# Seven-product values in an encoder layer: the first product's bank copies and the first keys' copies change places

## The chip, the cores and the metric

The kernel runs on 1 core of one Trainium2 chip. The metric is device time in microseconds (us) of one execution. In the text PE is TensorE (matmuls), ACT is ScalarE, DVE is VectorE, POOL is GpSimd, SP is the engine that issues most transfers. A bank is one PSUM tile of 128 partitions by 512 float32.

## The reference, cut to what matters

The program is a two-layer encoder over 512 tokens of width 1024. The change lies in layer 0, in the input projection of the neighbourhood attention, which makes queries, keys, values and a gate from the normed tokens `xn`:

```python
def mixer_na(xn, w_in, rpb, w_out):
    B, S, _ = xn.shape
    hd = NA_HEADS * NA_HEAD_DIM
    q, k, v, z = jnp.split(xn @ w_in, 4, axis=-1)
    shp = (B, S, NA_HEADS, NA_HEAD_DIM)
    o = neighbourhood_attention(q.reshape(shp), k.reshape(shp), v.reshape(shp), rpb)
    return (o.reshape(B, S, hd) * jax.nn.silu(z)) @ w_out
```

After it come the gated per-layer embedding, a second layer with latent attention, and a last norm. All of that is the same in both kernels.

## The kernel before, in words

Every float32 operand of a matmul is split in two parts, `hi` (a rounded copy, cast by ACT) and `lo` (what is left, subtracted by DVE or POOL), and a product is three kinds of matmul: hi by hi, lo by hi, hi by lo. So a weight tile costs a load (SP), a cast (ACT) and a subtraction (DVE in `piece`, line 240, POOL in `load_w`, line 89). Both write through three buffers each of `wraw`, `whi` and `wlo`.

`values_seven` makes the values with seven block products instead of eight. Products 1, 2 and 4 take quarters of the transposed tokens as they stand; products 7, 5, 6 and 3 take mixes of quarters. A mix (`mix`, line 255) is a DVE sum in place on the tokens (`xT<-xT`, 128x1024), an ACT cast (`V<-xT`) and a DVE subtraction (`V<-xT,V`). The mixes 6 and 3 hang together: the sum of 3 reads what the sum of 6 wrote. The weights of products 7, 6 and 4 are made in one tile `W7` by adding further pieces to it one after the other (`sums`, seen as `W<-W,wraw`).

A product is 24 matmuls on two banks, in four blocks of six: first chunk on bank 0, first chunk on bank 1, second chunk on bank 0, second chunk on bank 1. Products 1, 7 and 6 open two banks each (kinds `S`, `T` and `mm`); 2 goes on in the banks of 1, 4 in those of 7, 5 and 3 in those of 6. So before product 2 writes, the result of product 1 must be copied out: `after1(0)` and `after1(1)`, two ACT copies `s<-ps_S`. In the same way `after6` copies out of the banks of 6 (`s<-ps_mm`) before product 5 writes them, and `after7` adds to those of 7 and copies them.

Between the products stand the queries and keys of the first two head pairs, 0 and 1: `pair.load(j)` brings two weight tiles with `load_w`, `pair.products(j)` is 48 matmuls (24 for queries, 24 for keys) on the two `mm` banks, `pair.queries(j)` and `pair.keys(j)` are the copies out of these banks: for keys four ACT copies (`da` twice, `db` twice) and two DVE subtractions (`la`, `lb`). There are only two `mm` banks: the keys of pair 1 take the bank of the keys of pair 0, product 6 takes those of pair 1.

The order on ACT and DVE of all calls through `self.act` and `self.dve` is the order in which `values_seven` writes them (class `InOrder`, whose line 51 therefore stands beside all of them in the profile). The casts of `load_w` (line 100) go past this class, and a scheduler places them. The matmuls of the products stand in written order too (line 302 in the profile for the seven products, line 407 for queries and keys).

Of the kernel before, what the change touches and what calls it, by code (L numbers as in the profile page):

```python
# [56 lines left out]
class Trunk:  # L57
# [209 lines left out]
    def values_seven(self, pool, xT, xk, Q, pair, more):  # L267
# [14 lines left out]
        def left(p, s, k, i):  # L282
            if p in X:
                return X[p][:, 2 * s + k // 2, k % 2 * 256 + i * P:k % 2 * 256 + (i + 1) * P]
            half, t = {1: (0, i), 2: (1, i), 4: (1, 2 + i)}[p]
            return xT[s][half][:, k, t * P:(t + 1) * P]
# [4 lines left out]
        def product(p):  # L291
            for i in range(2):
                if p in banks:
                    C[p, i] = self.psum(banks[p])
            for c in range(2):
                for i in range(2):
                    ps = C[base.get(p, p), i]
                    m = [(left(p, s, k, i), W[p][c][r][:, k % 2 * S:(k % 2 + 1) * S])
                         for s, r in ((0, 0), (1, 0), (0, 1)) for k in (2 * c, 2 * c + 1)]
                    for j, (l, r) in enumerate(m):  # L300
                        with self.tc.issue_after(self.last_mm.ins):
                            self.last_mm = nc.tensor.matmul(ps, l, r, start=c == 0 and j == 0 and p in banks,  # L302
                                                            stop=c == 1 and j == 5 and p in (2, 3, 4),
                                                            skip_group_check=True)
# [4 lines left out]
        def copy(name, i, ps):  # L309
            t = kept(name, i)  # L310
            self.act.activation(t, ps, AF.Copy)
            return t
# [4 lines left out]
        def after1(i):  # L317
            s1[i] = copy("s1", i, C[1, i])
# [18 lines left out]
        def mixed(p):  # L337
            X[p], rest = self.mix(xk, p)
            return rest
# [8 lines left out]
        pair.queries(0)  # L348
        rest5 = mixed(5)
        product(1)  # L350
        p21 = self.piece(None, self.raw_piece(0, 3))
        rest5()
        W[2].append(p21())
        rest6 = mixed(6)
        pair.keys(0)
        pair.load(1)
        rest6()
        mixed(3)()
        more()
        after1(0)  # L360
        after1(1)
        made(7, 0, T[7][:, 0, :], True)
        product(2)
        out(0, 0, 0, C[1, 0])
# [1086 lines left out]
```

## Time and profile before

| | |
|---|---|
| median of 3 runs | 673.18 us (672.94 to 673.78) |
| the profiled execution, own time | 673.3 us |
| its span, first to last instruction | 671.5 us |
| outside the span | 1.8 us |
| PE busy in the span | 644.4 us (96%) |
| ACT, DVE, POOL busy | 451.5, 441.1, 413.3 us |
| mean granted PE clock | 0.982 |

In rows of the timeline the first number is the start in us from the span's start, the second the duration in us, then engine, line, operation, output<-inputs, and xN for N instructions merged in one row. In square brackets is the time for which the engine sat idle before the row, and what released it. A row of the windows view gives start:end, length, then for each engine its busy time and, in brackets, how many instructions ran; at the end stand the granted PE clock, the busy share of the transfer engines and GB/s.

### The profile page before, as it was taken

What the parts mean: (1) busy time and instruction counts of PE and PEld (TensorE: products, weight loads), DVE (VectorE), ACT (ScalarE), POOL (GpSimd) and SP (SyncE); (2) the same over time, 40 slices, a digit from 0 to 9 for tenths busy, and PEclk for the clock granted to TensorE, in tenths of its full rate; (3) what the DMA queues carried; (4) which work ended last, traced back from release to release, by engine and by line L of the source; (5) the groups of instructions that cost most, each with busy time, mean ns of one, the idle gap of its engine ahead of it and who ended that gap; (6) DMA issues with size and microseconds to landing.
All of it is one profiled execution on the core that took longest, in us unless ns stands there. A gap on an engine that the chain in (4) does not pass through costs nothing.

```text
span 671.5 us, 9963 instructions
## 1 busy us (share of the span) xinstructions
PE 644.4 (96%) x3299; PEld 544.2 (81%) x3299; DVE 441.1 (66%) x898; ACT 451.5 (67%) x887; POOL 413.3 (62%) x373
## 2 busy tenths in 40 slices
PE   9996599998999999999999999999999999999994
PEld 6884488787888888888899888888888888888884
DVE  6197587467787652667861723688888886474675
ACT  7574455686877774378754544887989898536855
POOL 0463101775887874389844744685978978436974
PEclk9998699998999999999999999999999999999997
DMA  9849344655995897745644425320121213583524
GB/s 331 330 160 287 104 138 129 221 131 163 231 244 166 217 246 201 280 158 188 192 149 130 138 71 148 96 68 9 56 64 63 64 48 125 191 327 126 173 78 157
DMA packets 46131, 107.41 MB, mean 160 GB/s; under 512 B 4736, under 2 KB 17792, under 8 KB 46080
## 3 DMA queue, kind: packets, MB, share of 16 engines
q1 hardware_dynamic: 34608, 87.12, 38.7%
q0 software_dynamic: 11040, 18.88, 13.2%
q10 hardware_dynamic: 432, 0.79, 0.3%
q8 instruction: 26, 0.43, 0.3%
q14 instruction: 25, 0.20, 0.1%
HBM read 95.23 MB, written 25.17 MB: 179 GB/s over the span
## 4 chain that ended last, share of the span: by engine, by line
PE 85%; DVE 1%; ACT 1%; POOL 1%; issue 0%; POOLq 0%; ACTq 0%
PE ps_mm L123 27%; PE ps_S L123 10%; PE ps_mm L935 6%; PE ps_T L155 6%; PE ps_T L827 5%; PE ps_O L1047 4%; PE ps_mm L827 3%; PE ps_S L827 3%; PE ps_O L584 2%; PE ps_mm L302 2%; PE ps_T L123 2%; PE ps_O L123 2%; PE ps_mm L885 2%; PE ps_T L302 2%; PE ps_mm L407 2%; PE ps_T L572 2%
## 5 line engine op out<-in xcount | busy, mean ns | idle before, releaser
L101 POOL TENSOR_TENSOR wwlo<-wraw,wwhi 128x1024 fp32r<-128x1024 f32 (+5 forms) x70 | 125.7, 1806 | 107.7 <-ACT wwhi L100 90.9
L100 ACT ACTIVATE wwhi<-wraw 128x1024 fp32r<-128x1024 f32 (+5 forms) x73 | 57.2, 806 | 45.5 <-PE ps_mm L123 19.3
L772 POOL TENSOR_TENSOR wlo<-wraw,whi 128x512 fp32r<-128x512 f32 x56 | 72.6, 1330 | 21.4 <-ACT whi L770 16.6
L1032 POOL TENSOR_TENSOR ex<-ex,rc 128x512 f32<-128x512 f32 x64 | 66.2, 1043 | 25.8 <-DVE rc L1031 22.0
L1030 ACT ACTIVATE ex<-ps_S,mx 128x512 f32<-128x512 f32 x64 | 44.0, 688 | 11.6 <-DVE mx L1028 10.1
L558 POOL TENSOR_TENSOR ex<-ex,rc 128x128 f32<-128x128 f32 (+1 forms) x64 | 37.4, 674 | 22.0 <-DVE rc L554 21.2
L1028 DVE TENSOR_REDUCE mx<-ps_S 128x1 f32<-128x512 f32 x64 | 43.7, 683 | 8.3 <-PE ps_S L123 7.7
L112 DVE TENSOR_TENSOR pt_lo<-ps_T,pt_hi 128x512 fp32r<-128x512 f32 x64 | 43.2, 682 | 7.2 <-ACT pt_hi L110 6.6
L110 ACT ACTIVATE pt_hi<-ps_T 128x512 fp32r<-128x512 f32 x64 | 37.8, 596 | 3.4 <-PE ps_T L155 3.0
L155 PE MATMUL ps_T<-ident,ex 128*128 128x128 f32 x256 | 38.3, 272 | 0.0
L155 PEld LDWEIGHTS ps_T<-ident,ex 128*128 128x128 f32 x256 | 31.5, 140 | 7.5
L123 PE MATMUL ps_mm<-xh,wwhi 128*128 128x512 f32 x120 | 35.1, 417 | 1.3 <-DVE Q L51 1.3
L552 ACT ACTIVATE ex<-ex,mx 128x128 f32<-128x128 f32 (+1 forms) x64 | 30.1, 473 | 9.0 <-DVE mx L542 8.7
L221 DVE TENSOR_TENSOR u<-ps_O,u 64x512 f32<-64x512 f32 x32 | 21.9, 685 | 20.4 <-ACT u L220 19.9
L123 PE MATMUL ps_mm<-xl,wwhi 128*128 128x512 f32 x120 | 32.1, 396 | 0.0
L770 ACT ACTIVATE whi<-wraw 128x1024 fp32r<-128x1024 f32 x28 | 29.3, 1057 | 3.3 <-DMA wraw<-sum 2.4
L123 PE MATMUL ps_mm<-xh,wwlo 128*128 128x512 f32 x120 | 31.5, 395 | 0.0
L123 PE MATMUL ps_S<-ko,qo 128*128 128x512 f32 x96 | 28.9, 409 | 0.0
L123 PE MATMUL ps_S<-ke,qe 96*128 96x512 f32 x96 | 28.6, 406 | 0.0
L935 PE MATMUL ps_mm<-cT,wwhi 128*128 128x512 f32 x94 | 27.7, 393 | 0.0
L220 ACT ACTIVATE u<-ps_O 64x512 f32<-64x512 f32 x32 | 18.9, 590 | 11.7 <-PE ps_O L584 8.4
L225 POOL TENSOR_TENSOR u<-u,z 128x512 f32<-128x512 f32 x16 | 22.2, 1386 | 7.2 <-DVE u L221 7.2
(482 smaller groups left out, 1925.4 us busy)
## 6 DMA issues: line engine op xcount, KB each, us to landing
sum<-gate POOLq DMA_DIRECT2D x12, 1024.0 KB, 8.3
wraw<-na_qk SPq DMA_DIRECT2D x16, 512.0 KB, 4.3
wraw<-sum SPq DMA_DIRECT2D x16, 512.0 KB, 3.3
pe<-pe SPq DMA_DIRECT2D x31, 256.0 KB, 6.6
wraw<-gate SPq DMA_DIRECT2D x12, 512.0 KB, 3.3
wraw<-na_v SPq DMA_DIRECT2D x10, 512.0 KB, 3.3
sum<-sum POOLq DMA_DIRECT2D x4, 1024.0 KB, 10.4
wraw<-na_o SPq DMA_DIRECT2D x8, 512.0 KB, 4.9
```

The source lines that it names most:

```text
L100: nc.scalar.activation(hi[:, c], raw[:, c], AF.Copy)
L101: f = lambda e, c=c: e.tensor_tensor(out=lo[:, c], in0=raw[:, c], in1=hi[:, c].bitcast(F32), op=ALU.subtract)
L110: self.last_copy = self.act.activation(hi, src, AF.Copy, scale=scale)
L112: self.dve.tensor_tensor(out=lo, in0=src, in1=hi.bitcast(F32), op=ALU.subtract)
L123: last = self.last_mm = nc.tensor.matmul(out, l, r, start=i == 0, stop=i == n - 1)
L155: self.last_mm = self.nc.tensor.transpose(t[:, i * P:(i + 1) * P], b, self.ident)
L772: nc.gpsimd.tensor_tensor(out=lo[:, o], in0=raw[:, o], in1=hi[:, o].bitcast(F32), op=ALU.subtract)
L827: mm = nc.tensor.matmul(ps, l, r, start=j == 0 and p in banks, stop=j == 11 and p in (2, 3, 4), skip_group_check=True)
L935: self.last_mm = nc.tensor.matmul(PS[key], *terms[i], start=i == 0, stop=i == len(terms) - 1)
L1028: nc.vector.reduce_max(mx, sp, axis=AX.X, negate=True)
L1030: nc.scalar.activation(ex, sp, AF.Exp, bias=mx, accum_out=sm)
L1032: nc.gpsimd.tensor_tensor(out=ex, in0=ex, in1=rc.to_broadcast([P, S]), op=ALU.mult)
```

## The change

The two copies out of the first product's banks are now written right behind that product: the first ahead of the cast of a weight piece of product 2, the second behind that cast. The loads for pair 1 are written ahead of mix 6. Mixes 6 and 3 stand together, their two subtractions behind both, and the copies of the first keys come after them. No operation is added or taken away.

```diff
         pair.queries(0)
         rest5 = mixed(5)
         product(1)
+        after1(0)
         p21 = self.piece(None, self.raw_piece(0, 3))
+        after1(1)
         rest5()
         W[2].append(p21())
+        pair.load(1)
         rest6 = mixed(6)
+        rest3 = mixed(3)
+        rest6()
+        rest3()
+        more()
         pair.keys(0)
-        pair.load(1)
-        rest6()
-        mixed(3)()
-        more()
-        after1(0)
-        after1(1)
         made(7, 0, T[7][:, 0, :], True)
         product(2)
         out(0, 0, 0, C[1, 0])
```

On ACT, from the cast of mix 5 to the cast of the first piece of `W7`. `V` is a mix's cast, the `whi` from `wraw` is the piece of product 2, the `wwhi` are the two weight tiles of pair 1, `s` are the copies out of product 1. Before:

```order
L51 ACTIVATE V_611<-xT 128x1024
L51 ACTIVATE whi<-wraw 128x1024
L100 ACTIVATE wwhi<-wraw 128x1024
L51 ACTIVATE V_648<-xT 128x1024
L51 ACTIVATE da<-ps_mm 64x512 x2
L51 ACTIVATE db<-ps_mm 64x512 x2
L51 ACTIVATE V_672<-xT 128x1024
L51 ACTIVATE s_677<-ps_S 128x512
L51 ACTIVATE s_679<-ps_S 128x512
L51 ACTIVATE whi<-W_519 128x1024
L100 ACTIVATE wwhi<-wraw 128x1024
```

and now:

```order
L51 ACTIVATE V_611<-xT 128x1024
L51 ACTIVATE s_639<-ps_S 128x512
L51 ACTIVATE whi<-wraw 128x1024
L51 ACTIVATE s_646<-ps_S 128x512
L100 ACTIVATE wwhi<-wraw 128x1024
L51 ACTIVATE V_664<-xT 128x1024
L51 ACTIVATE V_667<-xT 128x1024
L51 ACTIVATE da<-ps_mm 64x512
L100 ACTIVATE wwhi<-wraw 128x1024
L51 ACTIVATE da<-ps_mm 64x512
L51 ACTIVATE db<-ps_mm 64x512 x2
L51 ACTIVATE whi<-W_519 128x1024
```

The copies `s` moved from behind three mix casts and four key copies to the second and fourth place; the key copies moved behind both remaining mix casts, and the second `wwhi` now stands among them.

On DVE, from the subtraction of product 2's piece to that of the first piece of `W7`, with the numbers of the buffers. Before:

```order
L51 TENSOR_TENSOR xT_165<-xT_165,xT_164 128x4x256
L51 TENSOR_TENSOR la0_508<-ps_mm_551,da_650 64x512
L51 TENSOR_TENSOR lb0_509<-ps_mm_551,db_651 64x512
L51 TENSOR_TENSOR V6_648<-xT_165,V6_648 128x1024
L51 TENSOR_TENSOR xT_165<-xT_165 128x4x256
L51 TENSOR_TENSOR V3_672<-xT_165,V3_672 128x1024
```

and now:

```order
L51 TENSOR_TENSOR xT_165<-xT_165,xT_164 128x4x256
L51 TENSOR_TENSOR xT_165<-xT_165 128x4x256
L51 TENSOR_TENSOR V6_664<-xT_165,V6_664 128x1024
L51 TENSOR_TENSOR V3_667<-xT_165,V3_667 128x1024
L51 TENSOR_TENSOR la0_508<-ps_mm_551,da_673 64x512
L51 TENSOR_TENSOR lb0_509<-ps_mm_551,db_674 64x512
```

The first keys' `la` and `lb`, which end the use of their bank, moved from second and third place to the end. On SP and POOL the order is the same as before. On ACT one cast of a later weight tile (line 100) also changed places with a copy of product 5. On PE only the first head's eight score matmuls, which stood inside product 6, now stand together ahead of it.

## The prediction

> **What bounds the kernel now.** First the page's busy line, then its slices, then the windows around the place of the change, then the waits there.
>
> ```profile
> PE 644.4 (96%) x3299; PEld 544.2 (81%) x3299; DVE 441.1 (66%) x898; ACT 451.5 (67%) x887; POOL 413.3 (62%) x373
> PE   9996599998999999999999999999999999999994
> 60.80:74.36 13.56, 0.02 (x1) 0.00 (x0) 8.86 (x8) 5.76 (x9) 2.62 (x1) 0.61 0.87 217
> 74.36:81.35 6.99, 6.99 (x25) 5.67 (x26) 2.35 (x4) 3.04 (x4) 1.79 (x1) 0.78 0.00 0
> PE ps_S L302 <- ACT s L51: 13.5, 1, 13.5
> ```
>
> PE bounds the kernel, with one hole, slices 4 and 5. In it PE does nothing from 60.80 to 74.36, and what ends the wait is the copy `s` out of product 1's banks. The next window is product 2: 6.99 us at a granted clock of 0.78. At full clock 24 such matmuls take 5.44 us (the second row below), so the hole costs 13.54 + 1.55 = 15.1 us in all.
>
> ```profile
> 74.36 1.22 PE L302 MATMUL ps_S<-whi,xh 128*128 128x512 f32 x2 [13.54 <-ACT s L51]
> 92.39 5.44 PE ps_T L302 x24
> 81.51 10.88 PE ps_mm L407 x48
> 60.21 0.61 PE L302 MATMUL ps_S<-wlo,xh 128*128 128x512 f32 x2
> 58.85 0.62 PE L302 MATMUL ps_S<-wlo,xh 128*128 128x512 f32 x2
> ```
>
> The last two rows end the two banks of product 1, at 60.82 and 59.47. Why the copies come so late is seen on ACT, DVE and POOL:
>
> ```profile
> 58.48 1.06 ACT L51 ACTIVATE V<-xT 128x1024 fp32r<-128x1024 f32 x1 [4.63 <-DVE xT L51]
> 59.44 1.04 ACT L51 ACTIVATE whi<-wraw 128x1024 fp32r<-128x1024 f32 x1
> 60.39 1.04 ACT L100 ACTIVATE wwhi<-wraw 128x1024 fp32r<-128x1024 f32 x1
> 67.58 1.20 ACT L51 ACTIVATE db<-ps_mm 64x512 fp32r<-64x512 f32 x2
> 72.63 1.06 ACT L51 ACTIVATE V<-xT 128x1024 fp32r<-128x1024 f32 x1 [3.85 <-DVE xT L51]
> 73.71 1.09 ACT L51 ACTIVATE s<-ps_S 128x512 f32<-128x512 f32 x2
> 60.71 1.29 DVE L51 TENSOR_TENSOR wlo<-wraw,whi 128x512 fp32r<-128x512 f32 x2
> 61.92 3.36 DVE L51 TENSOR_TENSOR xT<-xT 128x1024 f32<-128x1024 f32 x1
> 71.38 1.22 DVE L51 TENSOR_TENSOR xT<-xT 128x1024 f32<-128x1024 f32 x1
> 61.58 2.62 POOL L101 TENSOR_TENSOR wwlo<-wraw,wwhi 128x1024 fp32r<-128x1024 f32 x1 [3.61 <-ACT wwhi L100]
> ```
>
> The rows of POOL and of line 101 matter: the same sum `xT<-xT` takes 1.22 us alone and 3.36 us while POOL subtracts.
>
> **The copies, moved up.** ACT is done with mix 5's cast at 59.54, the first bank is ready at 59.47: copy 59.6 to 60.15 (1.09 us for two, so 0.55 each), the piece's cast (1.04) to 61.2, second copy to 61.75. Product 2 then starts behind product 1 at 60.85. It needs bank 1 after six matmuls (1.36 us, a quarter of 5.44), at 62.2, and has it. Its third block, at 63.6, needs the `lo` of its second piece: cast 61.2 plus 1.29, so 62.5. It ends at 66.3 instead of 81.35, **15.05 us earlier**. The queries of pair 1 (half of 10.88) run to 71.7.
>
> **The first keys, moved back.** What is late next is the bank of the first keys, which the keys of pair 1 want at 71.7. DVE sums mix 6 from 62.5 to 63.7. POOL gets its cast (second copy 61.75, then 1.04) at 62.9, while DVE sums. I assume that it comes in between the two sums, since that of mix 3 has to wait for the end of that of mix 6. Then POOL holds 63.7 to 66.1, the price being 2.40 us from an undisturbed row:
>
> ```profile
> 79.56 2.40 POOL L101 TENSOR_TENSOR wwlo<-wraw,wwhi 128x1024 fp32r<-128x1024 f32 x1 [15.36 <-ACT wwhi L100]
> 39.74 4.29 DVE L1210 TENSOR_TENSOR xl<-xT,xh 128x512 fp32r<-128x512 f32 x7
> 41.92 4.37 POOL L101 TENSOR_TENSOR wwlo<-wraw,wwhi 128x1024 fp32r<-128x1024 f32 x1 [2.94 <-PE ps_S L123]
> ```
>
> Mix 3's sum ends at 67.3, its cast at 68.4; then `da`, the second `wwhi`, `da`, `db`, `db` (4 x 0.6 + 1.0) to 71.8, and `la`, `lb` (0.69 each) to **73.2**. The second `wwhi` is held by nothing else: its buffer is free after product 2's second block at 63.6, and POOL's `lo` of it, 70 to 72.4, is wanted by the last eight of the keys' 24 matmuls, at 76.9. SP's order and POOL's don't change. So a new wait of 1.55 us takes part of the place of the old one; pair 1's keys run 73.3 to 78.7, product 7 to 84.1. The bounds from rows: without any clash `lb` ends 2.4 earlier and there is no wait; as a second 2.4 us, if POOL came ahead of both sums and again behind, it ends at 75.6.
>
> [...]
>
> **The chain that then sets the time.** Behind `lb` DVE has fixed work up to the second keys' `lb`, which frees the bank that product 6 wants second. Rows of before that give its steps, start to start:
>
> ```profile
> 84.33 1.22 DVE L51 TENSOR_TENSOR W<-W,wraw 128x1024 f32<-128x1024 f32 x1
> 86.68 1.29 DVE L51 TENSOR_TENSOR wlo<-W,whi 128x512 fp32r<-128x512 f32 x2 [1.13 <-ACT whi L51]
> 87.89 1.22 DVE L51 TENSOR_TENSOR W<-W,wraw 128x1024 f32<-128x1024 f32 x1
> 89.14 0.69 DVE L51 SCALAR_TENSOR_TENSOR sa<-ps_mm,sa 64x512 fp32r<-64x512 f32 x1
> 90.86 1.29 DVE L51 TENSOR_TENSOR wlo<-W,whi 128x512 fp32r<-128x512 f32 x2
> 92.07 2.35 DVE L51 TENSOR_TENSOR W<-W,wraw 128x1024 f32<-128x1024 f32 x2
> 94.87 0.68 DVE L51 TENSOR_TENSOR la<-ps_mm,da 64x512 fp32r<-64x512 f32 x1 [0.45 <-ACT db L51]
> 95.57 0.69 DVE L51 TENSOR_TENSOR lb<-ps_mm,db 64x512 fp32r<-64x512 f32 x1
> ```
>
> Two pairs `wlo` for W7's halves 2.42 (1.21 each, 86.68 to 87.89); two `Q` 1.4 (priced as two `lb`); sum 1.22; the wait for a cast between sum and `wlo` 1.13, which stays; `wlo` 1.21; sum 1.25; `sa` to the next `wlo` 1.72 (89.14 to 90.86); `wlo` 1.21; two sums 2.35; `la`, `lb` 1.4. Together 15.3, so the second `lb` ends at 73.2 + 15.3 = 88.5; before it was 96.26. **That is 7.8 us earlier, not 15**: of the hole's gain DVE can pass on only half, because in before it had been waiting for PE meanwhile, and now PE waits for it. The data come in time: `W7` itself lands 11.3 us after 54.2, at 65.5, and is wanted at 71.8; the raw piece whose buffer POOL frees last, at 72.4, needs 3.1 to 8.8 us, and its sum stands at 84.8:
>
> ```profile
> wraw<-na_v SPq DMA_DIRECT2D x1, 512.0 KB, 8.8
> wraw<-na_v SPq DMA_DIRECT2D x1, 512.0 KB, 3.1
> 54.21 1.44 POOL L276 DMA_DIRECT2D W<-na_v  x1 [5.64 <-DMA W<-na_v]
> W<-na_v POOLq DMA_DIRECT2D x1, 1024.0 KB, 11.3
> ```
>
> PE: product 7 ends 84.1, eight score matmuls (0.12 us each in the last row below, 1 us), product 6's first block to 86.4, wait to 88.6 (**2.2 us**), product 6 ends at 92.7. From the second `lb` on, DVE and ACT keep their order and wait only for one another, so the copies before product 5 move by the same 7.8 (the second one, and the matmuls that wait for it):
>
> ```profile
> 104.94 0.60 ACT L51 ACTIVATE s<-ps_mm 128x512 f32<-128x512 f32 x1 [1.66 <-DVE ps_T L51]
> 105.59 1.20 PE L302 MATMUL ps_mm<-whi,V 128*128 128x512 f32 x4
> 99.19 0.12 PE ps_S L535
> ```
>
> Product 5's first block starts with the first copy at 95.5 (wait **2.8**), its second at 97.8 instead of 105.59 (wait **0.9**). From there PE has no hole of its own and everything it reads has moved by the same 7.8. The account on PE: +13.54 +1.55 −1.55 −2.2 −2.8 −0.9 = +7.6, plus 0.15 for the wait that product 5 had already: 7.8.
>
> **The clock.** Three new waits of 1.5 to 2.8 us lie close together. The nearest row for such a wait:
>
> ```profile
> 155.45 0.39 PE L584 MATMUL ps_O<-pl,Q 128*128 128x256 f32 x1 [2.11 <-DVE pl L112]
> 157.15 3.04 PE L123 MATMUL ps_mm<-xh,wwhi 128*128 128x512 f32 x8
> ```
>
> After 2.11 us idle eight matmuls took 3.04 us, where eight of the 48 in 10.88 take 1.81: 1.2 us lost, and some more in the transposes ahead. A slow clock in product 6 is hidden by the wait for the copies; in product 5 its first block has 0.9 us of cover. I take 0.4 of loss between 0 and 1.7 (the 1.55 of product 2, which had no cover). [...]
>
> **The sum.** 673.3 (the profiled execution, 0.1 above the median) − 7.8 + 0.4 = **665.9 us**.
>
> **The rivals.**
> *DVE keeps POOL out between the sums.* The `xl` rows speak for it: POOL issued at 41.92 and took 4.37, since DVE went through its subtractions without a pause. Against: there no instruction waited for the one ahead, mix 3's sum does, and at 61.92 POOL did win. Then mix 3's sum ends at 64.9, POOL works against the mixes' subtractions, the first `lb` ends near 71.2, POOL's second pass (to 72) costs W7's `lo` some 0.8: 1.2 better in all, 664.7.
> *The full gain.* If DVE's work from 73 to 88 had slack, 15.1 would carry: 658.2. Against: the steps above sum without slack.
> *The tail takes some back.* PE reaches the heads 8 us earlier, and a wait like that at 155 grows, or the slow clock falls on product 5 without cover: gain 3 to 6, 667.5 to 670. For it: ACT and POOL are busy 67% and 62% of the span; against: they have moved by the same 7.8.
> *The clock stays low, and it is slower.* One mechanism: the waits in 71.7 to 97.8 put PE to half clock, and it does not return before product 3 ends. Products 5, 4 and 3 are 16.3 us of full-speed work, each at half clock costs as much again: 665.5 + 16.3 = 681.8. It decides from 9.1 us of such work (40 matmuls) on. Against: after 13.54 us idle the clock was back within one product.
> *The hole only changes its name.* Had something else been nearly as late as the copies, product 2 would wait for it: but its piece's `lo` is ready at 62.0 in before. Same time, 673.
>
> **Chances.** Forecast 58% (665.4 to 667.2 with the clock's bounds), DVE keeps POOL out 15%, full gain 4%, tail 14%, same 4%, slower 5%. A measurement here can tell about 0.2% from no change, 1.3 us. Faster: 58 + 15 + 4 + 14 = 91%; same 4%; slower 5%. The range takes the forecast, the first rival down to no clash at all (2.4 better, 663.4), and half of the tail: 663.4 to 668.2.
>
> **What would show it.** Right: product 2 with no wait at about 61, no product above 5.6 us there; mix 3's `xT` at 3 to 3.6 us beside a `wwlo`; PE waits for DVE `lb` of 1.5 us at 72 and 2 us at 87, for ACT `s` of 3 us at 93; product 5's second block at 97 to 99. Wrong: PE without holes from 61 to 121 (the full gain), a wait over 2 us at 72, or a second block of product 5 at 98 and an end that is not 7 to 8 us earlier, which would put the loss in the heads.

## The result, and the profile after

| | before | changed |
|---|---|---|
| median | 673.48 us (672.94 to 674.66, 4 runs) | 664.79 us (664.01 to 664.85, 4 runs) |
| ratio, 95% interval | | 0.9866 [0.9849, 0.9883] |
| span of the profiled execution | 671.5 us | 662.2 us |
| first matmul of the heads' projection | 123.48 us | 115.26 us |

The changed kernel is 8.7 us faster; 665.9 us was forecast. The page of the changed kernel, PE's share, its slices and its granted clock:

```profile
PE 642.2 (97%) x3299; PEld 541.4 (82%) x3299; DVE 441.5 (67%) x898; ACT 451.3 (68%) x887; POOL 414.0 (63%) x373
PE   9999969989999999999999999999999999999994
PEclk9999999999999999999999999999999999999998
```

The hole in slices 4 and 5 is gone. The windows view of the changed kernel over the stretches of the prediction, and two more behind them:

```profile
60.80:74.36 13.56, 12.35 (x56) 9.92 (x54) 11.07 (x12) 10.14 (x14) 5.53 (x2) 1.00 0.96 249
74.36:81.35 6.99, 6.99 (x32) 5.82 (x31) 5.83 (x9) 2.14 (x3) 0.00 (x0) 1.00 0.29 98
81.35:92.23 10.88, 9.08 (x44) 7.26 (x42) 10.37 (x16) 6.23 (x9) 0.00 (x0) 1.00 0.43 145
92.23:104.08 11.85, 8.66 (x37) 6.60 (x36) 9.42 (x15) 7.31 (x10) 0.83 (x1) 1.00 0.23 71
```

PE now works where it stood still, at full clock, and has got holes further on: 1.8 us before 92.23 and 3.2 us before 104.08. In the third window DVE is busy 10.37 of 10.88 us. PE's rows of the timeline of the changed kernel, the first of product 2 and then those ahead of which it was idle:

```profile
60.66 0.62 PE L302 MATMUL ps_S<-whi,xh 128*128 128x512 f32 x2
72.91 2.06 PE L408 MATMUL ps_mm<-xh,wwhi 128*128 128x512 f32 x8 [1.22 <-ACT Q L51]
88.18 1.15 PE L302 MATMUL ps_mm<-whi,V 128*128 128x512 f32 x4 [1.80 <-DVE lb L51]
94.95 1.20 PE L302 MATMUL ps_mm<-whi,V 128*128 128x512 f32 x4 [2.45 <-ACT s L51]
97.35 1.21 PE L302 MATMUL ps_mm<-whi,V 128*128 128x512 f32 x4 [0.74 <-ACT s L51]
115.26 1.86 PE L123 MATMUL ps_mm<-xh,wwhi 128*128 128x512 f32 x7 [1.27 <-DVE Q L51]
```

Product 2 follows product 1 without a wait. The old wait of 13.54 us has four small ones in its place: pair 1's keys at 72.9, product 6 at 88.2, product 5 at 95.0 and 97.4. The heads' projection, the row at 115.26, stood here in before:

```profile
123.48 1.85 PE L123 MATMUL ps_mm<-xh,wwhi 128*128 128x512 f32 x7 [1.28 <-DVE Q L51]
```

What the four wait for is on DVE, ACT and POOL of the changed kernel:

```profile
62.43 4.56 DVE L51 TENSOR_TENSOR xT<-xT 128x1024 f32<-128x1024 f32 x2
71.38 0.68 DVE L51 TENSOR_TENSOR la<-ps_mm,da 64x512 fp32r<-64x512 f32 x1 [2.03 <-ACT db L51]
72.07 0.69 DVE L51 TENSOR_TENSOR lb<-ps_mm,db 64x512 fp32r<-64x512 f32 x1
87.34 0.69 DVE L51 TENSOR_TENSOR lb<-ps_mm,db 64x512 fp32r<-64x512 f32 x1
94.31 0.59 ACT L51 ACTIVATE s<-ps_mm 128x512 f32<-128x512 f32 x1
96.70 0.60 ACT L51 ACTIVATE s<-ps_mm 128x512 f32<-128x512 f32 x1 [1.80 <-DVE ps_T L51]
62.77 3.14 POOL L101 TENSOR_TENSOR wwlo<-wraw,wwhi 128x1024 fp32r<-128x1024 f32 x1 [5.04 <-ACT wwhi L100]
```

The first keys' `lb` ends at 72.76 and the matmul at 72.91 follows it (the row names an ACT copy as releaser; where `lb` came earlier, in two experiments below, this wait is gone). The second keys' `lb` ends at 88.03, and product 6 goes on at 88.18. The copies `s` out of product 6's banks end at 94.90 and 97.30, and the two blocks of product 5 start at 94.95 and 97.35.

### The profile page after: what moved, and what is told of

The parts are those of the page before. It is cut to its first block, busy times and chain, and to the rows that moved or that the text cites. A ratio compares the mean times of both kernels' runs of the same rounds, so it can differ in the third digit from the quotient of the medians.

```text
span 662.2 us, 9964 instructions
## 1 busy us (share of the span) xinstructions
PE 642.2 (97%) x3299; PEld 541.4 (82%) x3299; DVE 441.5 (67%) x898; ACT 451.3 (68%) x887; POOL 414.0 (63%) x373
## 4 chain that ended last, share of the span: by engine, by line
PE 88%; DVE 6%; ACT 3%; issue 1%; POOL 1%; DMA 0%; POOLq 0%; ACTq 0%; DVEq 0%
PE ps_mm L123 27%; PE ps_S L123 12%; PE ps_mm L936 7%; PE ps_T L155 6%; PE ps_T L828 5%; PE ps_O L1048 4%; PE ps_mm L828 3%; PE ps_S L828 3%; PE ps_T L123 2%; PE ps_O L123 2%; PE ps_O L585 2%; DVE wlo L51 2%; PE ps_mm L886 2%; PE ps_mm L200 2%; PE ps_T L573 1%
```

## The experiments

The time at which the heads' projection starts is used beside the medians, since the profiles give it to 0.1 us and the medians of the kernel before lie between 673.2 and 673.7.

### The copies alone

```diff
         product(1)
+        after1(0)
         p21 = self.piece(None, self.raw_piece(0, 3))
+        after1(1)
 ...
         mixed(3)()
         more()
-        after1(0)
-        after1(1)
         made(7, 0, T[7][:, 0, :], True)
```

> Only the two copies of product 1 move up; mixes, loads and first keys stand as before. The changed kernel has product 5's second block at 97.35 us and the first matmul of the heads' projection at 115.26 (before: 105.59 and 123.48). Theory (the DVE and ACT chain sets the time): product 2 starts at 60.7 without a wait, the first keys' lb ends near 68.5 so the wait for their bank is gone, but mix 3's sum comes later and DVE ends its work before the second keys about 1.1 us later: product 5's second block at 98.5, the heads at 116.4, 665.9 us. Rival (the wait of 1.2 us for the first keys' bank is what the change still pays on PE): without it PE is 1.2 us earlier than in the changed kernel all the way, second block at 96.1, 663.6 us.

Measured: 666.56 us (665.77 to 667.58), ratio 0.9897 [0.988, 0.9914] to before. Rows of PE, DVE and POOL from the timeline of this kernel:

```profile
90.31 2.05 PE L302 MATMUL ps_mm<-whi,V 128*128 128x512 f32 x4 [3.66 <-DVE lb L51]
117.39 1.85 PE L123 MATMUL ps_mm<-xh,wwhi 128*128 128x512 f32 x7 [1.28 <-DVE Q L51]
67.74 0.69 DVE L51 TENSOR_TENSOR lb<-ps_mm,db 64x512 fp32r<-64x512 f32 x1
68.47 3.06 DVE L51 TENSOR_TENSOR V<-xT,V 128x1024 fp32r<-128x1024 f32 x1
89.47 0.69 DVE L51 TENSOR_TENSOR lb<-ps_mm,db 64x512 fp32r<-64x512 f32 x1
68.04 2.40 POOL L101 TENSOR_TENSOR wwlo<-wraw,wwhi 128x1024 fp32r<-128x1024 f32 x1 [2.16 <-ACT wwhi L100]
```

The first keys' bank is free 4.3 us earlier than in the changed kernel and the wait for it is gone, yet the kernel is slower. The rival, by which this wait was what was left to pay, falls. What counts is when DVE is through: the second `lb` ends at 90.16 instead of 88.03, and product 6 waits 3.66 us. This `lb` comes 2.1 us later than in the changed kernel, where 1.1 were expected, and the heads start at 117.39 (116.4 expected), 2.1 us later as well. The expectation doesn't name what the rows show: POOL's second subtraction (68.04) meets mix 6's subtraction here, which takes 3.06 us, while the changed kernel has 2.43 us for both mixes' subtractions.

### The mixes and keys alone

```diff
         product(1)
-        after1(0)
         p21 = self.piece(None, self.raw_piece(0, 3))
-        after1(1)
 ...
         pair.keys(0)
+        after1(0)
+        after1(1)
         made(7, 0, T[7][:, 0, :], True)
```

(This diff is against the changed kernel.)

> Only mixes, loads and first keys move; the two copies of product 1 stay last, behind the keys. Theory: the copies end near 71.5 instead of 74.8, product 2 starts near 71.3 after a hole of about 10.5 us and still meets the slow clock (6.9 us instead of 5.44); the chain behind it then waits for PE again, product 5's second block near 102.2, about 670 us. Rival (the order of the keys and mixes has no worth of its own): hole of 13.5 as before, 673.3 us.

Measured: 669.56 us (669.03 to 669.81), ratio 0.9942 [0.9928, 0.9957]. PE's rows:

```profile
70.65 1.22 PE L302 MATMUL ps_S<-whi,xh 128*128 128x512 f32 x2 [9.91 <-ACT s L51]
79.08 1.98 PE L408 MATMUL ps_mm<-xh,wwhi 128*128 128x512 f32 x8
121.20 1.86 PE L123 MATMUL ps_mm<-xh,wwhi 128*128 128x512 f32 x7 [1.27 <-DVE Q L51]
70.65:76.82 6.17, 6.17 (x15) 4.82 (x16) 2.03 (x4) 2.43 (x3) 0.32 (x1) 0.50 0.32 96
```

The order of keys and mixes gives 3.7 us of the median by itself, because it brings forward the copies behind it. Not all of that is the hole: the hole is 3.6 us shorter, but product 2 now takes 8.4 us (70.65 to 79.08), not the 6.9 that were expected, since 6.2 us of it lie in the half clock (the last row). So the heads start only 2.3 us earlier than in before, and product 5's second block starts at 103.33 (102.2 expected). The rest of the gain in the profiles is the clock inside the heads: 1.00 over 141.80 to 161.80 here, 0.91 in before (last section). The copies alone are worth 6.7 us, both parts 8.7, less than the sum of the two: with the copies alone PE ends up waiting for DVE, and in this kernel ACT's copies still hold up product 2.

### POOL kept off the mixes' sums

```diff
             f = lambda e, c=c: e.tensor_tensor(out=lo[:, c], in0=raw[:, c], in1=hi[:, c].bitcast(F32), op=ALU.subtract)
+            if blank:
+                f = lambda e, c=c: e.memset(lo[:, c].bitcast(F32), 0.0)
 ...
-                weights[j] = [self.load_w(a["na_qk"][i + j], 1024) for i in (0, 8)]
+                weights[j] = [self.load_w(a["na_qk"][i + j], 1024, blank=i == 0) for i in (0, 8)]
```

> The changed kernel, with POOL filling the low part of pair 1's query weights with zeros instead of subtracting, which reads nothing; so the hi by lo term of these queries is left out of the result, the matmuls stay. Theory (POOL's subtraction blocks mix 3's sum, because both read SBUF): the two sums take 2.4 us together instead of 4.56, the first keys' lb ends at 70.5 instead of 72.8, no wait for their bank, the second keys' lb at 85.8 instead of 88.0, product 5's second block at 95.1, about 662.6 us. Rival (the sum is slow for its own form or its dependence on the other sum): sums stay 4.5 us, no change, 664.8 us.

Measured: 662.86 us (662.63 to 663.12), ratio 0.9844 [0.9829, 0.9859]. Rows of DVE and PE:

```profile
62.47 2.48 DVE L51 TENSOR_TENSOR xT<-xT 128x1024 f32<-128x1024 f32 x2
70.05 0.69 DVE L51 TENSOR_TENSOR lb<-ps_mm,db 64x512 fp32r<-64x512 f32 x1
85.32 0.69 DVE L51 TENSOR_TENSOR lb<-ps_mm,db 64x512 fp32r<-64x512 f32 x1
95.33 1.20 PE L304 MATMUL ps_mm<-whi,V 128*128 128x512 f32 x4 [0.74 <-ACT s L51]
113.22 1.86 PE L125 MATMUL ps_mm<-xh,wwhi 128*128 128x512 f32 x7 [1.28 <-DVE Q L51]
```

The same two sums, in the same order and form, take 2.48 us instead of 4.56 without POOL's subtraction. The zeros don't run beside the sums: with no cast to wait for, POOL writes them at 58.28, in 0.95 us, ahead of both. So the run shows that POOL's subtraction costs the sums 2.1 us, not what a POOL instruction that only writes would do beside them. The reason that the theory names, that both read SBUF, was not tried apart. The first `lb` ends at 70.74, no wait for its bank is left, and 2.0 us arrive at product 5's second block and at the heads. So the 2.1 us that POOL's subtraction puts between the sums pass to the heads undiminished, and the median falls by 1.9.

### One sum less, one sum more

The two kernels take away, or do twice, one sum of 1.22 us between the first and the second keys:

```diff
         raws = [self.raw_piece(0, 2 + c) for c in both]
         sums(T[7], 0, raws[0])
-        sums(T[7], 1, raws[1])
```

```diff
         sums(T[7], 0, raws[0])
+        sums(T[7], 0, raws[0])
         sums(T[7], 1, raws[1])
```

> The changed kernel without the last of the sums that make product 4's weights (1.22 us on DVE, so product 4 uses another weight). Theory (DVE's work between the first and the second keys sets the time): the second keys' lb 1.2 us earlier, at 86.8, product 5's second block at 96.1, the heads at 114.0, 663.6 us. Rival (PE's three waits each have a cause of their own on ACT): product 5's second block stays at 97.3 and the time at 664.8 us.

> The changed kernel with one of the sums of the last pair done twice (1.22 us more on DVE between the first and the second keys, so product 4 uses another weight). Theory: the second keys' lb 1.2 us later, at 89.2, product 5's second block at 98.6, the heads' projection at 116.5. Rival (slack behind the sums): product 5's second block stays at 97.3.

Measured: 663.19 us (662.71 to 663.91) with one less, ratio 0.985 [0.9835, 0.9864]; 666.5 us in the single run with one more. PE's rows, first with one less, then with one more:

```profile
73.28 2.08 PE L407 MATMUL ps_mm<-xh,wwhi 128*128 128x512 f32 x8 [1.32 <-ACT Q L51]
87.42 1.15 PE L302 MATMUL ps_mm<-whi,V 128*128 128x512 f32 x4 [0.64 <-DVE lb L51]
94.19 1.34 PE L302 MATMUL ps_mm<-whi,V 128*128 128x512 f32 x4 [2.45 <-ACT s L51]
96.59 2.06 PE L302 MATMUL ps_mm<-whi,V 128*128 128x512 f32 x4 [0.21 <-ACT s L51]
115.35 1.86 PE L123 MATMUL ps_mm<-xh,wwhi 128*128 128x512 f32 x7 [1.27 <-DVE Q L51]
```

```profile
73.09 2.08 PE L409 MATMUL ps_mm<-xh,wwhi 128*128 128x512 f32 x8 [1.26 <-ACT Q L51]
89.62 1.17 PE L302 MATMUL ps_mm<-whi,V 128*128 128x512 f32 x4 [3.03 <-DVE lb L51]
98.80 1.20 PE L302 MATMUL ps_mm<-whi,V 128*128 128x512 f32 x4 [0.74 <-ACT s L51]
116.67 1.85 PE L123 MATMUL ps_mm<-xh,wwhi 128*128 128x512 f32 x7 [1.27 <-DVE Q L51]
```

Product 6's wait is 0.64, 1.80 and 3.03 us with one sum less, as many, and one more: steps of 1.16 and 1.23. With one more, all of it arrives at the heads (116.67; this execution runs 0.2 us late from 73.09 on). With one less, the execution runs 0.4 us late from 73.28 on; product 5's second block starts 0.8 us earlier (96.59, 96.1 expected), which is 1.1 without that lag. But its matmuls ran at half clock there (0.50 over 95.10 to 98.50; 2.06 us for four of them, 1.21 in the changed kernel): from this block to the heads it takes 18.76 us instead of 17.91, so the heads start no earlier (115.35, 114.0 expected). The median is 1.6 us below the changed kernel; so its other executions presumably did not all lose that, which no profile shows. The rival of waits with causes of their own on ACT falls.

### The changed kernel again

> The changed kernel once more, beside its successor. If the clock is the reason why its profiled execution ended 0.8 us before its median, this profile shows the heads' projection at 115.3 again, and from there to the end either 546.9 us as in the first profile, with no stretch of half clock, or about 1.1 us more with one. The median stays at 664.5 to 665.

Measured: 664.89 us (664.02 to 665.94), ratio 0.9866 [0.9849, 0.9882]. The heads' projection starts at 115.33. From there both take 26.5 us to the first of these windows; the rows are of the first profile and then of this one:

```profile
141.80:161.80 20.00, 17.89 (x102) 15.32 (x101) 16.59 (x40) 13.97 (x31) 14.08 (x16) 1.00 0.75 187
161.80:662.20 500.40, 490.83 (x2594) 418.87 (x2592) 328.46 (x683) 346.04 (x703) 346.01 (x310) 1.00 0.48 146
```

```profile
141.85:161.85 20.00, 17.90 (x95) 15.23 (x94) 15.78 (x39) 12.91 (x30) 12.61 (x15) 0.91 0.66 171
161.85:664.20 502.35, 492.44 (x2602) 420.13 (x2599) 329.17 (x685) 346.64 (x704) 347.54 (x312) 1.00 0.49 146
```

The first window holds the wait of 2.1 us inside the heads that before had at 155.45, in both executions. In the first profile the clock stays at 1.00 behind it, in the second it falls (0.91 over the 20 us), seven matmuls fewer are done in the stretch, and the rest takes 1.95 us longer (1.1 more in all were expected). Of these, 1.5 come at the fall; 0.3 more come near 413 us, where PE waits 0.5 us for a transfer (`qe<-rl`) instead of 0.26.

### DVE's and ACT's work in the order in which PE asks for it

```diff
         raws = [self.raw_piece(0, 2 + c) for c in both]
-        sums(T[7], 0, raws[0])
-        sums(T[7], 1, raws[1])
         pair.keys(1)
         made(5, 0, T[5][:, 0, :])
         product(7)
-        made(4, 0, T[7][:, 0, :], True)
+        made(5, 1, T[5][:, 1, :])
         after7(0)
         after7(1)
-        made(5, 1, T[5][:, 1, :])
         product(6)
-        made(4, 1, T[7][:, 1, :], True)
         after6(0)
+        sums(T[7], 0, raws[0])
         after6(1)
+        sums(T[7], 1, raws[1])
+        made(4, 0, T[7][:, 0, :], True)
+        made(4, 1, T[7][:, 1, :], True)
```

> The changed kernel with DVE's and ACT's work around products 7, 6 and 5 written in the order in which PE asks for it: the second keys' copies ahead of the two last sums, product 5's weight pieces ahead of the copies of product 7, the copies of product 6 ahead of product 4's pieces. No work is added or left out. Theory (DVE and ACT set the time there, and PE's waits at products 6 and 5 come from the order of that work, not from its sum): the second keys' lb ends near 86.3, product 6 waits 0.4 us instead of 1.8, product 5 no more than 1 us instead of 3.2, the heads' projection starts near 110.8 instead of 115.3, about 660.4 us. Rival (the work itself is the bound, so what is put later is late next): the waits move to products 4 and 3, the heads at 114 or later, 663.5 us or more.

Measured: **655.46 us** (654.64 to 657.68), ratio 0.9735 [0.9716, 0.9755] to before: 9.4 us faster than the changed kernel beside it (664.89). All of PE's waits that the view lists for this kernel, with total, number and longest:

```profile
PE ps_mm L408 <- ACT Q L51: 1.1, 1, 1.1
PE ps_S L536 <- DVE mx L546: 0.8, 1, 0.8
PE ps_T L1164 <- PEq L1441: 0.8, 1, 0.8
PE ps_mm L302 <- ACT s L51: 0.5, 1, 0.5
PE ps_mm L123 <- DVE Q L51: 0.4, 1, 0.4
```

The waits for `lb` ahead of product 6 and for `s` ahead of product 5 shrink from 1.8 and 3.2 to nothing and 0.5 us, and none turns up at products 4 and 3; so the order of DVE's and ACT's work was the bound, not its sum. The heads start here:

```profile
110.47 2.12 PE L123 MATMUL ps_mm<-xh,wwhi 128*128 128x512 f32 x8 [0.41 <-DVE Q L51]
```

That is 4.8 us earlier than in the changed kernel, 4.5 were expected. The other half of the gain was not: the wait of 2.1 us inside the heads is gone from the list, and with it any fall of the clock there (1.00 over 110.47 to 195.20): from the heads' start to the end it takes 543.2 us (653.7 of span less 110.47), against 546.9 and 548.9 in the two profiles of the changed kernel. The scheduler had placed the heads' instructions in another order on PE, ACT and DVE than in the changed kernel. That this new order removed the wait fits, but it was not tried apart.

## Why the prediction was right, point by point

- **The copies, moved up.** Right. Product 2 starts at 60.66 (worked out: 60.85) and takes 5.44 us, 60.66 to 66.10 from start to start.
- **The first keys, moved back, and POOL between the sums.** Right in each step: the two sums take 4.56 us, of which 2.08 are POOL's (2.48 without it), POOL's own row is 3.14 us (0.74 of waiting and 2.40), and `lb` ends at 72.76 (73.2). Why POOL gets in there, the dependence between the two sums as the prediction assumes, was not tried apart. The rival in which DVE keeps POOL out, the first of the list, did not occur.
- **DVE's fixed work of 15.3 us to the second `lb`.** Right: 72.76 to 88.03 is 15.27. It ends 8.2 us earlier than in before, 7.8 were forecast.
- **The four waits on PE.** Worked out as 1.55, 2.2, 2.8 and 0.9; the profile gives idle times of 1.22, 1.80, 2.45 and 0.74. These are not quite the same measure. The idle time begins when the last matmul has ended, 0.17 us after the next one could have started (rows of eight follow each other at 1.81 us and last 1.98), and the prediction counts from start to start. So counted, PE loses 1.38, 1.97, 2.61 and 0.92 us. The first three are some 0.2 shorter than forecast, since the first `lb` was put 0.4 us late and all behind it with it. The old wait is 13.70 us so counted (60.66 to 74.36), not the 13.54 with which the prediction's account on PE starts. The heads start 8.22 us earlier, against 7.8.
- **The clock.** This is the term that was mis-sized, and in its place as well. 0.4 us of loss at product 5 was taken (its upper bound of 1.7 is 0.15 more than the row it names); in both profiles of the changed kernel the clock is 1.00 through products 6 and 5, so there was none. In one experiment it did fall at the same place, to 0.50, and cost 0.85 us (one sum less). Why it falls in one execution and not in another was not shown (last section), so no single size was right. The loss that does vary sits in the heads: there the profiled execution of before paid for half clock (0.91 over 141.80 to 161.80) and the first one of the changed kernel did not (1.00). That is why the spans differ by 9.3 us (671.5 and 662.2) and the heads' starts by 8.22. That part of the difference is not shown to belong to the change: the second profile of the changed kernel paid as well.
- **The rivals.** *Full gain*: no, the four waits are there, and the runs with a sum less and more show that DVE's time passes through to product 6 and product 5 one to one, once each execution's own lag is taken off. *The tail takes some back*: no. *The clock stays low*: no. *The hole only changes its name*: no.
- **The sum.** The medians, 664.79 and 664.89, lie 1.1 us under the forecast. Of that 0.4 is the chain and 0.4 the clock at product 5; the rest, some 0.3, is within what the clock in the heads adds or leaves out from one execution to the next (1.5 us between the two profiles of the changed kernel).

## What to carry to other kernels

When a long wait on the bounding engine is removed, its gain is not the wait but how far the next engine's queue can follow: here 13.5 us of hole and 1.6 us of slow clock gave 8.2, since DVE had 15.3 us of work in a fixed order between two banks that PE needed. Adding that work up row by row gave the heads' start to half a microsecond. And once another engine's queue is what PE waits for, the next gain is to write that queue in the order in which PE asks: here with the same work 4.8 us more at the heads' start, and 9.4 in the median, with an order of the heads that came along with it.

## What the runs showed of the hardware that was not expected

The clock falls in some executions and not in others at one and the same wait. In all eight profiles other than that of the resorted kernel PE waits 2.1 us inside the heads. In five of them the clock falls in the 20 us that hold this wait, and from the heads' start to the end they take 548.0 to 548.9 us; in the other three it does not, and they take 546.4 to 546.9:

| profile | granted clock over 141.80 to 161.80 | from the heads' start to the end |
|---|---|---|
| before; the copies alone; no clash | 0.91; 0.91; 0.91 | 548.0; 548.0; 548.1 us |
| the changed kernel again; one sum more | 0.91; 0.91 | 548.9; 548.0 us |
| the changed kernel, first profile | 1.00 | 546.9 us |
| mixes and keys alone | 1.00 | 546.8 us |
| one sum less | 1.00 | 546.4 us |

The windows view over two stretches at a clock of 0.50, of before inside the heads, and of the copies alone at product 6:

```profile
155.94:159.34 3.40, 3.40 (x14) 2.92 (x13) 3.35 (x11) 3.20 (x10) 0.70 (x2) 0.50 0.50 160
```

```profile
89.30:96.10 6.80, 5.79 (x14) 4.56 (x15) 5.12 (x9) 2.64 (x4) 0.00 (x0) 0.50 0.40 134
```

In before the wait ends at 155.45, in the changed kernel's first profile at 147.23. The stretch of 3.41 us around the wait, and the 3.41 us behind it, in before and then in the changed kernel:

```profile
152.52:155.93 3.41, 1.30 (x12) 1.10 (x11) 3.38 (x6) 1.64 (x3) 2.18 (x1) 1.00 0.99 393
155.93:159.34 3.41, 3.41 (x14) 2.93 (x13) 3.35 (x11) 3.20 (x10) 0.70 (x2) 0.50 0.50 160
```

```profile
144.30:147.71 3.41, 1.30 (x12) 1.10 (x11) 3.38 (x6) 1.65 (x3) 2.18 (x1) 1.00 1.01 401
147.71:151.12 3.41, 3.41 (x22) 3.00 (x21) 3.35 (x11) 3.21 (x10) 0.70 (x2) 1.00 0.47 159
```

PE is busy 1.30 us of the first stretch in both, with 12 matmuls; behind it the clock is 0.50 in the one, with 14 matmuls, and 1.00 in the other, with 22. So the length of the wait (2.11 us in both), and PE's work beside it, don't tell the two apart, and what does was not shown: no experiment moved this wait alone. Nor was it shown for the two experiments in which the clock fell at products 6 and 5 (0.50 over 89.30 to 96.10 in the copies alone, over 95.10 to 98.50 with one sum less). What can be carried on is the size: between two executions of one kernel, the changed one, the fall makes a difference of 1.5 us.
